# Grouped instance norm on one core: the middle units moved in pairs, with 64 KB rows instead of 32 KB rows

## The chip, the core and the metric

The kernel runs on one core of a Trainium2 chip. Times are device microseconds (us) of one execution; the time before is the median of three executions, 626.96 us (626.79 to 627.2). Beside them stands one profiled execution, from which all durations are taken.

## The reference

The input is 4 x 8 x 16 = 512 channels of 256 x 256 float32 numbers (134 MB), and a gamma for each of 8 x 16 = 128 channels. Every channel is normalized by its own mean and variance and multiplied by its gamma:

```
mu = x.mean(axis=(3, 4), keepdims=True)
var = ((x - mu) ** 2).mean(axis=(3, 4), keepdims=True)
x_norm = (x - mu) / np.sqrt(var + 1e-5)
out = x_norm * gamma[None, :, :, None, None]
```

## The kernel before, in words

A *unit* is 16 channels, laid on 128 partitions: 8 partitions (S) for each channel, 8192 numbers (32 KB) on each partition, 4 MB in all. There are 32 units, and DRAM holds the rows of a unit one behind the other, so that loading or storing a unit is one DMA of 128 rows of 32 KB. Such a DMA runs on all 16 DMA engines, eight rows on each, and each engine signals when its eight are done.

Six slots of SBUF (line 45, `AHEAD = 6`) hold six units. Unit u lies in slot u % 6, is normalized in place, and is stored from there; the load of unit u + 6 into the slot (line 136) waits for that store to land. I write L5 for the load of unit 5 and S5 for its store.

Which queue issues what: the first six loads go out at once, L1 and L3 from ScalarE's queue, the others from SyncE's (SP); all later loads go out from SP's queue, in order (lines 47-48, 56-57, 136); all stores from ScalarE's queue (line 134), so that a store is issued behind the work that ScalarE has before it. Each of the two queues is served in order, and both run on the same 16 DMA engines.

What is done with a unit (lines 105 to 136): VectorE sums each row (line 107) while ScalarE sums the squares (line 108; the squares themselves go to `junk`, which nobody reads); TensorE adds the partial sums of a channel's eight partitions and spreads them to all eight by a matmul with `navg` (line 116); VectorE, ScalarE and VectorE again make variance, root, reciprocal and scale on 128 x 1 tiles (lines 117 to 127); VectorE applies mean and scale to the whole unit (line 130); ScalarE's queue issues the store. VectorE takes the units strictly one after the other.

Before the loop, GpSimd's queue writes a small block of zeros (`touch`, 16 rows of 512 B) into the output (line 54), where the first store writes over it later, and loads gamma (line 55); 60 no-ops are asked for on ScalarE (lines 59-60); GpSimd makes `navg` (lines 66 to 75); VectorE spreads gamma to a row (line 83), and eight small matmuls and a copy turn it into columns, one for each unit of a group of eight (lines 87 to 94).

The order on each engine is the order of the program text (`manual_schedule`).

Of the kernel before, what the change touches and what calls it, by code (L numbers as in the profile page):

```python
# [1 line left out]

# [4 lines left out]

F32 = mybir.dt.float32
U8 = mybir.dt.uint8
ALU = mybir.AluOpType  # L10
ACTF = mybir.ActivationFunctionType
AX = mybir.AxisListType


@with_exitstack
def kernel(
    ctx: ExitStack,
    tc: tile.TileContext,
    x: bass.AP,
    gamma: bass.AP,  # L20
    out: bass.AP,
):
    nc = tc.nc
    B, G, C, H, W = x.shape
    P = nc.NUM_PARTITIONS
    HW = H * W
    n_ch = B * G * C
    S = 8
    K = P // S
    F = HW // S  # L30
    U = n_ch // K
    NG = (G * C) // K
    AHEAD = 6
    assert HW % S == 0 and (G * C) % K == 0

    xv = x.rearrange("b g c h w -> (b g c h w)").rearrange("(u p f) -> u p f", p=P, f=F)
    ov = out.rearrange("b g c h w -> (b g c h w)").rearrange("(u p f) -> u p f", p=P, f=F)
    gv = gamma.rearrange("g c -> (g c)")

    data = ctx.enter_context(tc.tile_pool(name="data", bufs=1))  # L40
    singles = ctx.enter_context(tc.tile_pool(name="singles", bufs=1))
    psum = ctx.enter_context(tc.tile_pool(name="psum", bufs=4, space=bass.MemoryType.PSUM))
    ctx.enter_context(tc.manual_schedule())

    slots = [data.tile([P, F], F32, name=f"xt{i}") for i in range(AHEAD)]

    def load(u, queue):
        queue.dma_start(out=slots[u % AHEAD][:], in_=xv[u])  # L48


    g_row = singles.tile([1, G * C], F32, name="g_row")
    touch = singles.tile([16, 128], F32, name="touch")
    nc.vector.memset(touch[:], 0.0)  # L53
    nc.gpsimd.dma_start(out=ov[0][0::S, 0:128], in_=touch[:])  # L54
    nc.gpsimd.dma_start(out=g_row[:], in_=gv[None, :])  # L55
    for u in range(AHEAD):
        load(u, nc.scalar if u in (1, 3) else nc.sync)

    for _ in range(60):
        nc.scalar.nop()  # L60

    eps_t = singles.tile([P, 1], F32, name="eps_t")
    nc.gpsimd.memset(eps_t[:], 1e-5)
    one = singles.tile([1, 1], F32, name="one")
    nc.gpsimd.memset(one[:], 1.0)
    navg = singles.tile([P, K, S], F32, name="navg")
    nc.gpsimd.memset(navg[:], -1.0 / HW)  # L67
    nc.gpsimd.affine_select(  # L68
        out=navg[:], in_=navg[:], pattern=[[-S, K], [0, S]], compare_op=ALU.is_ge,
        fill=0.0, base=0, channel_multiplier=1,  # L70
    )
    nc.gpsimd.affine_select(  # L72
        out=navg[:], in_=navg[:], pattern=[[S, K], [0, S]], compare_op=ALU.is_ge,
        fill=0.0, base=S - 1, channel_multiplier=-1,
    )
    navg_w = navg[:].rearrange("p k s -> p (k s)")
    root_eps = singles.tile([P, 1], F32, name="root_eps")
    nc.scalar.activation(out=root_eps[:], in_=eps_t[:], func=ACTF.Sqrt)  # L78
    g_rep = singles.tile([1, NG, K, S], F32, name="g_rep")
    g_ps = psum.tile([P, NG], F32, name="g_ps", bufs=1)  # L80
    g_col = singles.tile([P, NG], F32, name="g_col")

    nc.vector.tensor_copy(  # L83
        out=g_rep[:],
        in_=g_row[:].rearrange("o (n k) -> o n k", n=NG).unsqueeze(3).to_broadcast([1, NG, K, S]),
    )
    for n in range(NG):
        nc.tensor.matmul(  # L88
            out=g_ps[:, n : n + 1],
            lhsT=g_rep[:, n].rearrange("o k s -> o (k s)"),  # L90
            rhs=one[:],
            start=True, stop=True,
        )
    nc.vector.tensor_copy(out=g_col[:], in_=g_ps[:])  # L94

    junk = singles.tile([P, F], U8, name="junk")

    st = singles.tile([P, U, 2], F32, name="st")
    nvar = singles.tile([P, U], F32, name="nvar")
    std = singles.tile([P, U], F32, name="std")  # L100
    rstd = singles.tile([P, U], F32, name="rstd")
    scale = singles.tile([P, U], F32, name="scale")

    squares = []
    for u in range(U):
        t = slots[u % AHEAD]
        nc.vector.reduce_sum(out=st[:, u, 0:1], in_=t[:], axis=AX.X)  # L107
        square = nc.scalar.activation(  # L108
            out=junk[:], in_=t[:], func=ACTF.Square, accum_out=st[:, u, 1:2],
        )  # L110
        if u:

            tc.declare_no_dep(square.ins, squares[-1].ins, reason="junk, ordered by the root between")
        squares.append(square)
        ps = psum.tile([P, 2], F32, name="ps")
        nc.tensor.matmul(out=ps[:], lhsT=navg_w, rhs=st[:, u], start=True, stop=True)  # L116
        nc.vector.tensor_scalar(  # L117
            out=nvar[:, u : u + 1], in0=ps[:, 0:1], scalar1=ps[:, 0:1],
            scalar2=ps[:, 1:2], op0=ALU.mult, op1=ALU.add,
        )  # L120
        nc.scalar.activation(  # L121
            out=std[:, u : u + 1], in_=nvar[:, u : u + 1], func=ACTF.Sqrt,
            bias=eps_t[:], scale=-1.0,
        )
        nc.vector.reciprocal(out=rstd[:, u : u + 1], in_=std[:, u : u + 1])  # L125
        g = u % NG
        nc.vector.tensor_mul(  # L127
            out=scale[:, u : u + 1], in0=rstd[:, u : u + 1], in1=g_col[:, g : g + 1],
        )
        nc.vector.tensor_scalar(  # L130
            out=t[:], in0=t[:], scalar1=ps[:, 0:1], scalar2=scale[:, u : u + 1],
            op0=ALU.add, op1=ALU.mult,
        )
        nc.scalar.dma_start(out=ov[u], in_=t[:])
        if u + AHEAD < U:
            load(u + AHEAD, nc.sync)


# [1 line left out]
_INS = ['x', 'gamma']  # L140
_OUTS = [((4, 8, 16, 256, 256), 'float32')]


# [23 lines left out]
```

## Time and profile before

| | |
|---|---|
| median of three executions | 626.96 us |
| span of the profiled execution (its time outside of the span is not recorded) | 624.9 us |
| first and last data row on a DMA engine, from the span's start | 2.10 us, 623.90 us |
| moved | 268.46 MB in 64 transfers of 4 MB and two small ones |
| VectorE, ScalarE, TensorE busy | 71%, 38%, 3% of the span |
| one row of 32 KB on a DMA engine, median of 8192 | 1.213 us |

The profile's page gives the busy time of each engine, the span in 40 equal slices (the row named DMA is the busy share of the 16 DMA engines in tenths, 9 for 90% or more; below it what they moved), the queues (q1 is SP's, q10 ScalarE's, q0 GpSimd's), the groups of instructions, and how long the DMAs of each kind took from issue to landing. The trace also keeps a record of each row that a DMA engine moved, with queue, start, duration and size: 8192 rows of 32 KB, and 4-byte records, which are the signals that an engine's share of a DMA is done.

### The profile page before, as it was taken

The page shows a single profiled execution, that of the slowest core. Times are in us where ns is not written, and L with a number is a line of the kernel's source. Part 1 is how long each engine was busy: PE and PEld are TensorE (multiplying, and loading weights), DVE is VectorE, ACT ScalarE, POOL GpSimd, SP SyncE. Part 2 cuts the span into 40 slices and gives each one's busy share as a digit, 9 for nine tenths or more (in the row PEclk, how much of TensorE's full clock was granted, in tenths as well). Part 3 has the DMA queues.
Part 4 walks back from the last instruction along what each step waited for, and adds up shares of the span by engine and source line. Part 5 has one row for each costly group of instructions (what it writes and reads, how often), then busy time and mean ns, then how long its engine had stood idle before and what let it go on. Part 6 is the DMA issues. An engine that isn't in the chain of part 4 may idle for free.

```text
span 624.9 us, 631 instructions
## 1 busy us (share of the span) xinstructions
PE 21.4 (3%) x80; PEld 19.5 (3%) x80; DVE 443.4 (71%) x163; ACT 238.8 (38%) x98; POOL 2.4 (0%) x11
## 2 busy tenths in 40 slices
PE   0200000000000000000000000000000000000000
PEld 0200000000000000000000000000000000000000
DVE  0588999999776687666786767867668676687730
ACT  0444444444443234432344423444224442244400
POOL 1000000000000000000000000000000000000000
DMA  8999999999999999999999999999999999999998
GB/s 370 436 426 430 422 434 436 436 436 437 432 424 433 436 436 424 436 436 434 436 436 432 422 436 436 434 426 436 436 434 436 436 434 419 436 436 434 426 436 369
DMA packets 9282, 268.46 MB, mean 430 GB/s; under 512 B 1072, under 2 KB 1088, under 8 KB 1088
## 3 DMA queue, kind: packets, MB, share of 16 engines
q10 hardware_dynamic: 4896, 142.61, 52.9%
q1 hardware_dynamic: 4320, 125.83, 46.8%
q0 software_dynamic: 64, 0.01, 0.0%
q14 instruction: 2, 0.02, 0.0%
HBM read 134.22 MB, written 134.23 MB: 430 GB/s over the span
## 4 chain that ended last, share of the span: by engine, by line
another core or an unknown queue 61%; DMA 17%; DVE 15%; SPq 1%; PE 1%; issue 0%; ACT 0%
DVE st L107 10%; DMA xt<-in_x_dram 10%; DMA out_dram<-xt 8%; DVE xt L130 5%; SPq L48 1%; PE ps L116 1%; ACT std L121 0%; DVE nvar L117 0%; DVE rstd L125 0%; DVE scale L127 0%
## 5 line engine op out<-in xcount | busy, mean ns | idle before, releaser
L107 DVE TENSOR_REDUCE st<-xt 128x1 f32<-128x8192 f32 x32 | 277.9, 8685 | 100.4 <-DMA xt<-in_x_dram 100.4
L108 ACT ACTIVATE junk<-xt 128x8192 uint8<-128x8192 f32 x32 | 225.0, 7030 | 275.1 <-DMA xt<-in_x_dram 231.9
L130 DVE TENSOR_SCALAR xt<-xt,ps,scale 128x8192 f32<-128x8192 f32 x32 | 145.6, 4550 | 1.2
L121 ACT ACTIVATE std<-nvar,eps_t 128x1 f32<-128x1 f32 x32 | 9.4, 294 | 79.6 <-DVE nvar L117 79.6
L116 PE MATMUL ps<-st,navg 128*128 128x2 f32 x64 | 17.9, 349 | 557.1 <-DVE st L107 557.1
L116 PEld LDWEIGHTS ps<-st,navg 128*128 128x128 f32 x64 | 16.0, 311 | 558.9 <-issue 558.9
L117 DVE TENSOR_SCALAR nvar<-ps 128x1 f32<-128x1 f32 x32 | 9.2, 287 | 23.8 <-PE ps L116 23.8
L125 DVE RECIPROCAL rstd<-std 128x1 f32<-128x1 f32 x32 | 5.2, 164 | 11.6 <-ACT std L121 11.6
L83 DVE COPY g_rep<-g_row 1x1024 f32<-1x1024 f32 x1 | 0.7, 681 | 14.3 <-DMA g_row<-in_gamma_dram 14.3
L108 ACT ACTIVATION_READ_ACCUMULATOR junk<-xt 128x1 f32 x32 | 6.0, 186 | 0.0
L127 DVE TENSOR_TENSOR scale<-rstd,g_col 128x1 f32<-128x1 f32 x32 | 5.1, 159 | 1.1
L88 PE MATMUL g_ps<-one,g_rep 1*128 1x1 f32 x16 | 3.5, 347 | 16.1 <-DVE g_rep L83 16.1
L88 PEld LDWEIGHTS g_ps<-one,g_rep 1*128 1x128 f32 x16 | 3.5, 325 | 16.1 <-issue 16.1
L94 DVE COPY g_col<-g_ps 128x8 f32<-128x8 f32 x1 | 0.2, 166 | 3.7 <-PE g_ps L88 3.7
L78 ACT ACT_TABLE_LOAD x1 | 1.3, 1283 | 1.7 <-PEq L151 1.7
L53 DVE MEMSET touch<- 16x128 f32 x1 | 0.2, 165 | 0.9 <-PEq L151 0.9
L54 POOL DMA_DIRECT2D out_dram<-touch x1 | 0.6, 619 | 0.8 <-DVE touch L53 0.8
L55 POOL DMA_DIRECT2D g_row<-in_gamma_dram x1 | 0.5, 487 | 0.0
L68 POOL TENSOR_SCALAR_AFFINE_SELECT navg<-navg 128x128 f32<-128x128 f32 x1 | 0.4, 400 | 0.1
L72 POOL TENSOR_SCALAR_AFFINE_SELECT navg<-navg 128x128 f32<-128x128 f32 x1 | 0.4, 399 | 0.1
L67 POOL MEMSET navg<- 128x128 f32 x1 | 0.2, 232 | 0.0
L78 ACT ACTIVATE root_eps<-eps_t 128x1 f32<-128x1 f32 x1 | 0.2, 203 | 0.0
(6 smaller groups left out, 0.6 us busy)
## 6 DMA issues: line engine op xcount, KB each, us to landing
out_dram<-xt ACTq DMA_DIRECT2D x32, 4096.0 KB, 62.5
xt<-in_x_dram SPq DMA_DIRECT2D x30, 4096.0 KB, 38.5
xt<-in_x_dram ACTq DMA_DIRECT2D x2, 4096.0 KB, 31.5
out_dram<-touch POOLq DMA_DIRECT2D x1, 8.0 KB, 9.1
g_row<-in_gamma_dram POOLq DMA_DIRECT2D x1, 0.5 KB, 13.3
```

Source lines behind the costliest of these rows:

```text
L48: queue.dma_start(out=slots[u % AHEAD][:], in_=xv[u])
L78: nc.scalar.activation(out=root_eps[:], in_=eps_t[:], func=ACTF.Sqrt)
L83: nc.vector.tensor_copy(out=g_rep[:], in_=g_row[:].rearrange("o (n k) -> o n k", n=NG).unsqueeze(3).to_broadcast([1, NG, K, S]),)
L88: nc.tensor.matmul(out=g_ps[:, n : n + 1], lhsT=g_rep[:, n].rearrange("o k s -> o (k s)"), rhs=one[:], start=True, stop=True,)
L107: nc.vector.reduce_sum(out=st[:, u, 0:1], in_=t[:], axis=AX.X)
L108: square = nc.scalar.activation(out=junk[:], in_=t[:], func=ACTF.Square, accum_out=st[:, u, 1:2],)
L116: nc.tensor.matmul(out=ps[:], lhsT=navg_w, rhs=st[:, u], start=True, stop=True)
L117: nc.vector.tensor_scalar(out=nvar[:, u : u + 1], in0=ps[:, 0:1], scalar1=ps[:, 0:1], scalar2=ps[:, 1:2], op0=ALU.mult, op1=ALU.add,)
L121: nc.scalar.activation(out=std[:, u : u + 1], in_=nvar[:, u : u + 1], func=ACTF.Sqrt, bias=eps_t[:], scale=-1.0,)
L125: nc.vector.reciprocal(out=rstd[:, u : u + 1], in_=std[:, u : u + 1])
L127: nc.vector.tensor_mul(out=scale[:, u : u + 1], in0=rstd[:, u : u + 1], in1=g_col[:, g : g + 1],)
L130: nc.vector.tensor_scalar(out=t[:], in0=t[:], scalar1=ps[:, 0:1], scalar2=scale[:, u : u + 1], op0=ALU.add, op1=ALU.mult,)
```

## The change

The first six and the last six units stay as they are. The twenty between them become ten *wide* units: 32 channels, 4 partitions for each, 16384 numbers (64 KB) on each partition, 8 MB in one DMA of 128 rows of 64 KB. The six slots become three pairs of slots; a wide unit fills a pair, a narrow unit one half. There are 22 units now: 0 to 5 narrow, 6 to 15 wide, 16 to 21 narrow, and L and S count these from here on where the changed kernel is meant. A load is issued as soon as enough slots have been stored (`behind`): L6 behind S1, L7 behind S3, L8 behind S5, then L(u + 3) behind S(u) for wide ones, L16 and L17 behind S13, L18 and L19 behind S14, L20 and L21 behind S15.

A wide unit is summed in two halves on VectorE and ScalarE, and two matmuls add the halves in PSUM; the small steps, the apply (one instruction of 16384 numbers a partition) and the store come once for it. There are two `navg` matrices and two sets of gamma columns, one for each kind of unit. The block of zeros and the no-ops are gone.

```diff
-    slots = [data.tile([P, F], F32, name=f"xt{i}") for i in range(AHEAD)]
+    pairs = [data.tile([P, 2, F], F32, name=f"xt{i}") for i in range(SLOTS // 2)]
...
+    while at < total:
+        wide = 2 if ENDS <= at < total - ENDS else 1
+        units.append((at, wide, slot))
+        at += wide
+        slot = (slot + wide) % SLOTS
...
+    def on_chip(u):
+        at, wide, slot = units[u]
+        pair = pairs[slot // 2]
+        if wide == 2:
+            return pair[:].rearrange("p t f -> p (t f)")
+        return pair[:, slot % 2]
+
+    def in_dram(flat, u):
+        at, wide, slot = units[u]
+        return flat[at * K * HW : (at + wide) * K * HW].rearrange("(p f) -> p f", p=P)
...
     def load(u, queue):
-        queue.dma_start(out=slots[u % AHEAD][:], in_=xv[u])
-    touch = singles.tile([16, 128], F32, name="touch")
-    nc.vector.memset(touch[:], 0.0)
-    nc.gpsimd.dma_start(out=ov[0][0::S, 0:128], in_=touch[:])
+        queue.dma_start(out=on_chip(u), in_=in_dram(xf, u))
...
+    for u in range(U):
+        free += held[u]
+        while nxt < U and held[nxt] <= free:
+            free -= held[nxt]
+            behind[u].append(nxt)
+            nxt += 1
...
-    for _ in range(60):
-        nc.scalar.nop()
...
+    for wide in (1, 2):
+        s = S // wide
+        k = K * wide
+        ng = GC // k
+        m = singles.tile([P, k, s], F32, name=f"navg{wide}")
...
+        for h in range(wide):
+            part = t[:, h * F : (h + 1) * F]
+            nc.vector.reduce_sum(out=st[:, u, 2 * h : 2 * h + 1], in_=part, axis=AX.X)
+            square = nc.scalar.activation(
+                out=junk[:], in_=part, func=ACTF.Square, accum_out=st[:, u, 2 * h + 1 : 2 * h + 2],
+            )
...
+            nc.tensor.matmul(
+                out=ps[:], lhsT=navg[wide], rhs=st[:, u, 2 * h : 2 * h + 2],
+                start=h == 0, stop=h == wide - 1,
+            )
...
         nc.vector.tensor_scalar(
-            out=t[:], in0=t[:], scalar1=ps[:, 0:1], scalar2=scale[:, u : u + 1],
+            out=t, in0=t, scalar1=ps[:, 0:1], scalar2=scale[:, u : u + 1],
             op0=ALU.add, op1=ALU.mult,
         )
-        nc.scalar.dma_start(out=ov[u], in_=t[:])
-        if u + AHEAD < U:
-            load(u + AHEAD, nc.sync)
+        nc.scalar.dma_start(out=in_dram(of, u), in_=t)
+        for v in behind[u]:
+            load(v, nc.sync)
```

## The prediction, as it was put on record

> **What bounds the kernel now.** I read the page's slices first, then the stages, then the records of the single rows.
>
> ```profile
> PE 21.4 (3%) x80; PEld 19.5 (3%) x80; DVE 443.4 (71%) x163; ACT 238.8 (38%) x98; POOL 2.4 (0%) x11
> ...
> DMA  8999999999999999999999999999999999999998
> ...
> q10 hardware_dynamic: 4896, 142.61, 52.9%
> q1 hardware_dynamic: 4320, 125.83, 46.8%
> ...
> out_dram<-touch POOLq DMA_DIRECT2D x1, 8.0 KB, 9.1
> g_row<-in_gamma_dram POOLq DMA_DIRECT2D x1, 0.5 KB, 13.3
> ```
>
> No compute engine is full; the DMA engines are, from the first slice to the last, and the shares of q10 and q1 add up to 99.7%. The stages (us, busy time of PE, PEld, DVE, ACT, POOL, the clock's share, the DMA share, GB/s) say that no stage is different:
>
> ```profile
> 0.00:22.60 22.60, 3.54 (x16) 3.48 (x16) 1.01 (x3) 1.49 (x2) 2.40 (x11) 1.00 0.94 395
> 60.00:160.00 100.00, 3.92 (x14) 3.52 (x14) 89.46 (x36) 45.52 (x22) 0.00 (x0) 1.00 1.00 433
> 160.00:540.00 380.00, 11.15 (x40) 10.02 (x40) 274.16 (x100) 147.74 (x60) 0.00 (x0) 1.00 1.00 433
> 585.20:600.30 15.10, 0.56 (x2) 0.50 (x2) 13.85 (x5) 7.42 (x3) 0.00 (x0) 1.00 1.03 445
> ```
>
> So the time is 2.1 us to the first row, 621.8 us of full DMA engines, 1.0 us behind the last row: the span of 624.9; 2.05 us lie outside it up to the median of 626.96, which I carry over. A change can win only by making rows cheaper, and lose only by letting the DMA engines run dry. Where could they? At the end:
>
> ```profile
> 585.26 8.69 DVE L107 TENSOR_REDUCE st<-xt 128x1 f32<-128x8192 f32 x1 [4.35 <-DMA xt<-in_x_dram]
> 595.73 4.55 DVE L130 TENSOR_SCALAR xt<-xt,ps,scale 128x8192 f32<-128x8192 f32 x1
> 600.32 0.34 ACTq L134 DMA_DIRECT2D out_dram<-xt  x1
> ```
>
> The last load lands at 585.18; its unit is summed and applied, and its store goes out 15.1 us later. In the row records, stores land at 594.87, 604.55, 614.23 and 623.91: at 585.18 four stores were still to be moved, 9.68 us each. Three of them (29 us) cover the 15.1. **That cover is what the change touches.**
>
> In between, the row records show a load and a store landing together every 19.36 us: the two queues take turns, row by row, eight rows each, 19.36 / 16 = 1.21 us a row.
>
> **Is a turn a row, or so many bytes?** Each row of touch (512 B) took 27 ns, but its 4-byte signal ran 2.44 us after it, gamma's 32 B 2.42 us after that, its signal again 2.42: each time one 32 KB row of q1 and one of q10. That is also why 0.5 KB took 13.3 us to land. A queue with a small record loses its turn like one with 32 KB: turns go by record. The Trainium skill (DMA: Bandwidth & Descriptors, "Queues, rings and completion order") says the same, a round-robin that drains a whole packet before switching; it leaves open what a packet is for a 64 KB row, which no row here shows.
>
> **The change, part by part.**
>
> *Fewer, longer rows.* Twenty units of 8 + 8 rows an engine become 160 rows of 64 KB where there were 320 of 32 KB, and 20 signals an engine go: 180 records fewer. The fixed price of a record is not shown by itself. A whole 4-byte record takes 9 ns, so it is between 0 and 9 ns: 0 to 1.6 us won. I take the middle, 0.8 us. If records were waited for one by one, more would be won: by the fit of the Trainium skill (DMA: Bandwidth & Descriptors, "Anatomy of one DMA": about 2.0 us fixed for each DMA, plus bytes by 436 GB/s) twenty DMAs fewer would be worth 40 us. The trace disagrees: 8192 rows x 1.213 / 16 = 621 us fill the 621.8, so no fixed cost of a DMA is uncovered.
>
> *Wide stage.* L(u + 3) waits for S(u). A wide unit needs 38.7 us of load and 38.7 of store at half rate, and on VectorE 2 x 8.69 + 1.75 for the small chain + 2 x 4.55 = 28.2: together 105.6 against three pairs x 38.7 = 116, so one of the queues always has rows. VectorE (28.2 of 38.7), ScalarE (2 x 7.2) and TensorE stay beneath; the second half's square waits for the first on the same engine, nothing. Cost 0; cover gone at 10 us.
>
> *Entering it.* L6, L7 and L8 wait for two stores each, so q1 runs empty for some us before L8; q10 has S5, S6 queued, and one queue alone moves as much (0.98 to 1.03 DMA share behind 585.2, where q10 is alone). Cost 0. It fixes a phase, though: L8 is issued 0.41 us after S5 lands (row records to SP's issue) and a first row follows an issue by 1.3 to 2.2 us (0.80 to 2.10 and 2.97 at the start), while S6 starts at once with a 2.42 us row. Most engines give S6 two rows first, so when S6 lands, L8 still lacks two. From there they go in step: L(u + 2) lands 7.3 us after S(u).
>
> *Leaving it.* Now a 64 KB store row takes turns with 32 KB load rows, and stores get two thirds. From S13's landing, with 1.21 and 2.42 us a row:
> - L, S, L: L15 lands at 7.3. Then S14's other seven rows with six of L16: 24.2, S14 lands at 31.4.
> - S15 goes out 28.3 us after L15: 35.6, first row about 37.3; meanwhile five load rows alone. Eight rows of S15 with eight load rows: 29.0, S15 lands at 66.4. 19 load rows done of the 48 of L16 to L21.
> - 29 load rows and 28 store rows in turn, 57 x 1.21 = 69.0: L21 lands at 135.4. Of S16 to S20, 12 rows are left: 14.5 us, empty at 149.9.
> - S21 goes out at 135.4 + 15.1 = 150.5, first row 1.3 to 2.2 later. **All 16 engines are dry for 1.9 to 2.8 us**; the last one counts, so 2.8.
>
> Before, the 15.1 us had 29 us of cover; now 14.5.
>
> *Touch and no-ops.* ScalarE's issues end at 1.68 and its table load starts at 1.72: the 60 no-ops take nothing, nor does dropping them. Touch cost each engine 36 ns. Whether it warms the output for the first store is not shown; with it, the load rows beside S0's first took 1.6 to 1.9 instead of 1.21 us (41.58 us), and the first load rows of all 1.2 to 2.0. So dropping it costs -0.04 to 0.8 us; I take 0, since that delay stands already in the trace. S0 no longer waits for touch, which landed 27 us earlier.
>
> *Small work.* Three more instructions on GpSimd (1.0 us), 4 more gamma matmuls (0.44 us each with their weights, 1.8) and two copies: the chain ended at 19.9 and would at most end at 22.4, still before the first load (22.55); gamma also comes two turns earlier. If late, VectorE would start late, and S0 queues behind L3 till 41.98 anyway. In the loop 10 x 4 small VectorE and ScalarE steps go; they stand beside full DMA engines: 0.
>
> **Sum:** +2.8 (dry end) - 0.8 (records) = +2.0 on a span of 624.9, so 626.9, and 626.96 + 2.0 = **629.0**.
>
> **Rivals.**
> - *No overtaking.* A 64 KB row is cut into two records of 32 KB, or turns go by bytes: then the change does not do what it says, or does it without its price. Stores and loads stay level, at the last landing four stores are left as before, nothing runs dry: 626.96 - 0.1 (20 signals at most 9 ns) to - 0.8, 626.2 to 626.9. For it: all rows shown have one size. Against it: the 512 B and 4 B records that waited full turns. 0.20.
> - *Faster.* No overtaking, and each record that goes saves all of the 9 ns: 625.3. A 4-byte record would then be fixed price alone, which is the far end. 0.08. (That DMAs have a fixed cost which nothing covers, and so end far lower, gets no chance: it needs idle DMA engines, and there are none to 0.7 us in 621.8.)
> - *One row less of phase.* If L8's first row comes within S6's first 2.42 us on all engines (an arrival of 1.7 to 2.6 us, so some surely will not), one load row is left instead of two. Then S15 follows S14 almost at once, 17 load rows are done instead of 19, 31 are left against 30 store rows, S20 has 10 rows left: 12.1 us of cover, 4.3 to 5.2 us dry, 626.96 + 5.2 - 0.8 = 631.4. 0.10.
> - *Something slower that no row shows*, a 64 KB row that takes more than two of 32 KB: 1% more on 160 rows of 2.42 would be 3.9 us, on top. All 8192 rows but 83 took 1.205 to 1.230, so nothing points at it. 0.07.
>
> **How the numbers follow.** The forecast has 0.55, from 627.8 (a row more of cover, 1.21) to 630.2 (a row less). A measurement of this kernel can tell about 0.2%, 1.25 us: faster is beneath 625.7, slower above 628.2. Faster: 0.09. Same: no overtaking and the low edge of the forecast, 0.24. Slower: 0.67. The range, 625.7 to 631.5, takes in the forecast, the phase rival and no overtaking, and leaves out 0.15.
>
> **What would show it.** Right: records of 64 KB with about 2.42 us each; in the row records S14 and S15 landing some 30 us apart where wide stores before them are 38.7 apart; the last load landing 12 to 13 us later than 585.2; a DMA share well beneath 1 for some 3 us before the last store; the last store issued after the one before it has landed. Wrong: records of 32 KB alone; S14, S15 at 38.7; four stores left behind the last load; a dry stretch in the wide stage; 64 KB rows over 2.43 us; a first store whose rows take several us.

## The result, and the profile after

The changed kernel is slower: 638.34 us, median of four executions (634.03 to 639.94), beside 626.88; the ratio is 1.0171 with a 95% interval of 1.0143 to 1.0199. Six executions taken later give 637.78 (634.1 to 640.42) and 1.0169 (1.0146 to 1.0191). Executions of the kernel before lie within 0.8 us, those of the changed one within 6: already that points to something not repeatable at its end. The execution that was profiled took 639.94 us, the slowest of the four.

One thing about times: the row records, here and in the text ahead, are given 0.30 us later than on the profile's own clock (there the first row before starts at 1.80 us, not 2.10). Distances between rows are not touched by it, and the landings given here lie mostly within 0.1 us of the time at which their semaphore was seen. A distance from an issue to a first row is 0.30 us too long in the prediction (1.0 to 1.9 us, not 1.3 to 2.2); below, such distances are on the profile's clock.

The page of the changed kernel, span, slices, queues:

```profile
span 638.2 us, 566 instructions
...
DMA  9999999999999999999999999999999999999966
GB/s 380 442 394 433 450 413 409 454 448 421 423 448 427 431 436 427 431 439 411 456 398 460 407 448 444 411 452 407 448 417 429 417 419 407 435 429 429 431 301 265
...
q10 hardware_dynamic: 3456, 142.61, 51.9%
q1 hardware_dynamic: 2880, 125.83, 46.4%
```

Before, only the first and the last slice were under 9; now the last two stand at 6, and 301 and 265 GB/s were moved there. The records fell from 4896 and 4320 to 3456 and 2880: there are rows of 64 KB, as the change says, and the wide ones took 2.418 us in the median.

The stages of the changed kernel, cut at what the prediction named (S13 lands at 469.5, S14 at 501.1, S15 at 538.6, L21 at 610.8; the last column but one is the share of the DMA engines):

```profile
197.00:469.50 272.50, 7.83 (x28) 7.03 (x28) 186.94 (x42) 101.78 (x35) 0.00 (x0) 1.00 1.00 432
469.50:501.00 31.50, 1.12 (x4) 1.00 (x4) 25.37 (x6) 14.54 (x5) 0.00 (x0) 1.00 0.96 409
501.00:538.60 37.60, 1.11 (x4) 1.00 (x4) 27.81 (x11) 14.83 (x6) 0.00 (x0) 1.00 1.00 415
538.60:610.80 72.20, 1.67 (x6) 1.50 (x6) 42.75 (x16) 22.25 (x9) 0.00 (x0) 1.00 1.00 432
610.80:627.00 16.20, 0.56 (x2) 0.50 (x2) 13.85 (x5) 7.42 (x3) 0.00 (x0) 1.00 0.49 209
```

The last row is the one that matters. Before, the same 15 us between the last load and the last store's issue ran at a full share; here the DMA engines are half empty. The last narrow unit, in the timeline of the changed kernel:

```profile
610.91 8.69 DVE L154 TENSOR_REDUCE st<-xt 128x1 f32<-128x8192 f32 x1 [4.89 <-DMA xt<-in_x_dram]
...
621.39 4.55 DVE L178 TENSOR_SCALAR xt<-xt,ps,scale 128x8192 f32<-128x8192 f32 x1
...
625.97 0.34 ACTq L182 DMA_DIRECT2D out_dram<-xt  x1
```

S20 has landed at 624.15, 1.8 us before S21 is issued: the dry end that was forecast. What was not forecast stands in the row records. Here is when the first and the last of the 16 engines finished their share of a transfer:

```
                       first engine   last engine   apart
before, L31 (last load)      584.28        585.18    0.90
after,  L6                   115.56        117.49    1.93
after,  L17                  517.04        524.70    7.66
after,  L21 (last load)      601.13        610.84    9.71
after,  S20                  616.96        624.15    7.19
after,  S21 (last store)     636.86        637.02    0.16
```

A load has landed when the last engine is done. The records do not name their engine; rows are strung together by end and start to tell the 16 apart. One engine lags, and everything behind it waits: that engine is dry for 3.0 us (624.15 to 627.11), the typical one, done with S20 at 617 to 619, for some 9.

### The profile page after: what moved, and what is told of

It reads as the page before. It is cut to its first block, busy times and chain, and to the rows that moved or that the text cites. A ratio compares the mean times of both kernels' runs of the same rounds, so it can differ in the third digit from the quotient of the medians.

```text
span 638.2 us, 566 instructions
## 1 busy us (share of the span) xinstructions
PE 23.3 (4%) x88; PEld 21.3 (3%) x88; DVE 434.1 (68%) x124; ACT 235.9 (37%) x88; POOL 3.1 (0%) x13
## 3 DMA queue, kind: packets, MB, share of 16 engines
q10 hardware_dynamic: 3456, 142.61, 51.9%
q1 hardware_dynamic: 2880, 125.83, 46.4%
## 4 chain that ended last, share of the span: by engine, by line
DMA 59%; DVE 34%; another core or an unknown queue 2%; PE 1%; ACT 1%; issue 1%; SPq 0%
DMA xt<-in_x_dram 32%; DMA out_dram<-xt 27%; DVE st L154 22%; DVE xt L178 11%; PE ps L161 1%; ACT std L169 1%; DVE nvar L165 1%; DVE rstd L173 0%; DVE scale L175 0%; SPq L71 0%
## 5 line engine op out<-in xcount | busy, mean ns | idle before, releaser
L178 DVE TENSOR_SCALAR xt<-xt,ps,scale 128x8192 f32<-128x8192 f32 (+1 forms) x22 | 142.8, 6490 | 0.8
L169 ACT ACTIVATE std<-nvar,eps_t 128x1 f32<-128x1 f32 x22 | 6.5, 294 | 69.3 <-DVE nvar L165 69.3
L165 DVE TENSOR_SCALAR nvar<-ps 128x1 f32<-128x1 f32 x22 | 6.3, 287 | 16.4 <-PE ps L161 16.4
L173 DVE RECIPROCAL rstd<-std 128x1 f32<-128x1 f32 x22 | 3.6, 164 | 8.0 <-ACT std L169 8.0
L130 PE MATMUL g_ps<-one,g_all 1*128 1x1 f32 x24 | 5.4, 348 | 11.9 <-DVE g_all L125 11.9
L130 PEld LDWEIGHTS g_ps<-one,g_all 1*128 1x128 f32 x24 | 5.3, 324 | 11.9 <-issue 11.3
L175 DVE TENSOR_TENSOR scale<-rstd,g_col 128x1 f32<-128x1 f32 x22 | 3.5, 159 | 0.7
```

The costliest lines, as they stand in the source:

```text
L130: nc.tensor.matmul(out=g_ps[:, n : n + 1], lhsT=g_rep[:, n].rearrange("o k s -> o (k s)"), rhs=one[:], start=True, stop=True,)
L165: nc.vector.tensor_scalar(out=nvar[:, u : u + 1], in0=ps[:, 0:1], scalar1=ps[:, 0:1], scalar2=ps[:, 1:2], op0=ALU.mult, op1=ALU.add,)
L169: nc.scalar.activation(out=std[:, u : u + 1], in_=nvar[:, u : u + 1], func=ACTF.Sqrt, bias=eps_t[:], scale=-1.0,)
L175: nc.vector.tensor_mul(out=scale[:, u : u + 1], in0=rstd[:, u : u + 1], in1=g_cols[wide][:, g : g + 1],)
L178: nc.vector.tensor_scalar(out=t, in0=t, scalar1=ps[:, 0:1], scalar2=scale[:, u : u + 1], op0=ALU.add, op1=ALU.mult,)
```

## The experiments

Theory A is the forecast's: 64 KB store rows take two turns' worth of bytes beside 32 KB load rows, the loads fall behind while the wide stage is left, and the end runs dry. Rivals: B, pairs as such (a load that waits for two units); C, 64 KB rows are bad wherever they stand; D, the entry sets it.

**All rows 32 KB, pairs kept (e1).** The halves of a pair get 32 bytes between them, so that a wide row cannot be moved in one piece:

```diff
-    pairs = [data.tile([P, 2, F], F32, name=f"xt{i}") for i in range(SLOTS // 2)]
+    pairs = [data.tile([P, 2, F + 8], F32, name=f"xt{i}") for i in range(SLOTS // 2)]
...
-            return pair[:].rearrange("p t f -> p (t f)")
-        return pair[:, slot % 2]
+            return pair[:, :, 0:F]
+        return pair[:, slot % 2, 0:F]
```

> The changed kernel with each half of a pair of slots 32 bytes apart on the partition, so that every wide transfer keeps its place, its waits and its bytes but moves in rows of 32 KB instead of 64 KB. Theory A (a 64 KB store row against a 32 KB load row takes two thirds of the DMA engines, loads fall behind where the wide stage is left, and the last unit's store is late): all rows alike, no overtaking, four stores left behind the last load, 626 to 628.5. Theory B (pairs as such: a load waits for two units' stores, its queue runs empty, whatever the rows): 634 or more. Theory C (64 KB rows are slower or put the 16 engines out of step wherever they stand): 626 to 628.5, as A.

Measured: 629.91 (628.76 to 630.09), ratio 1.0043 (1.0028 to 1.0058). Some 8 of 11 us come back, so row size is most of the loss; 2.8 us stay, more than A allowed, with all rows alike.

**The two stores that meet narrow loads in 32 KB rows (e2).** The helper `parts` cuts a wide transfer into two, one half of each partition's row after the other:

```diff
+    cut_loads = ()
+    cut_stores = (14, 15)
+
+    def parts(u, cut):
+        return (slice(0, F), slice(F, 2 * F)) if cut else (slice(None),)
...
-        nc.scalar.dma_start(out=in_dram(of, u), in_=t)
+        for c in parts(u, u in cut_stores):
+            nc.scalar.dma_start(out=in_dram(of, u)[:, c], in_=t[:, c])
```

> The changed kernel, but the stores S14 and S15, the two wide ones that meet narrow loads, go out as two transfers of 32 KB rows each, one half of every partition's row after the other; the other eight wide units keep 64 KB rows. Theory A: the overtaking is gone where it costs, nearly the whole loss comes back, 626.5 to 630. Theory B: 634 or more. Theory C: at most the two units' share of the loss comes back, 634 or more.

Measured: 630.48 (629.49 to 633.39), ratio 1.0064 (1.0044 to 1.0084). Two stores of 22 bring back 7 to 8 us, though the median lies just over A's 630. The stretch between the last load (589.22, the engines 0.9 us apart) and the issue of the last store, in this kernel's stages:

```profile
589.20:604.30 15.10, 0.56 (x2) 0.50 (x2) 13.78 (x5) 7.42 (x3) 0.00 (x0) 1.00 1.02 437
```

The share is full again. So most of the loss hangs on the leaving of the wide stage, and rows of 64 KB elsewhere cost little between these medians (0.6 us beside e1): this speaks for A, against B, and leaves C a small part at most. It does not separate the dry end from slower rows, since both go together here; e7 does. What is left, 3.4 us, is about what e1 left.

**The three loads that meet narrow stores in 32 KB rows (e3).** `cut_loads = (6, 7, 8)`, nothing else.

> The changed kernel, but the loads L6, L7 and L8, the wide ones that meet narrow stores where the wide stage is entered, go out as two transfers of 32 KB rows each; leaving the wide stage is untouched. Theory A: the loss stays, 633 to 640. Theory B: it stays, 633 to 640. A theory D, that the delay and the phase of the entry set the loss (S6 lands 197 us where 192 was worked out): below 632.

Measured: 655.73 (650.04 to 661.46), ratio 1.0489 (1.0434 to 1.0544): none of the theories. The slices of its page show where it went, 160 to 230 us:

```profile
GB/s 388 421 421 421 453 421 431 443 421 439 352 373 336 354 388 453 429 429 437 425 453 392 437 453 433 408 453 437 412 441 418 437 427 402 445 425 429 443 327 265
```

The entry itself became smooth (each half of L6 to L8 waits for one store only, and loads and stores land together each 19.4 us until 158.8). Then S6 and S7, in 64 KB rows beside the cut loads, took 3.1 us a row in the mean instead of 2.42, for 70 us. So D is not settled by it, but one thing is: cutting rows on one queue alone can be worse than on none.

**The kernel before without the block of zeros and the no-ops (e4).**

```diff
-    touch = singles.tile([16, 128], F32, name="touch")
-    nc.vector.memset(touch[:], 0.0)
-    nc.gpsimd.dma_start(out=ov[0][0::S, 0:128], in_=touch[:])
...
-    for _ in range(60):
-        nc.scalar.nop()
```

> The kernel before without the block of zeros and without the no-ops, nothing else changed. The prediction has this part at 0 (between -0.04 and 0.8 us): 626.9, at most 627.7. Were the block what keeps the first store quick: over 628.

Measured: 627.2 (626.66 to 627.53), ratio 1.0001 (0.9991 to 1.0010). This part is 0.

**Both ends cut (e5).** `cut_loads = (6, 7, 8)`, `cut_stores = (6, 7, 14, 15)`: no wide row stands beside a narrow one.

> The changed kernel with 32 KB rows, as two transfers of one half each, wherever a wide transfer meets a narrow one: loads L6, L7, L8 (each half then waits for one narrow store only, so that the load queue does not run empty at the entry), stores S6 and S7, which meet those loads, and S14 and S15. From L9 and S8 to L15 and S13 rows stay at 64 KB on both queues. If the loss comes from rows of unlike size side by side and from the entry's empty load queue, both are gone: 626 to 628. If 64 KB rows by themselves cost (slow, or out of step), six wide units still have them: 630 or more.

Measured: 631.05 (630.17 to 631.87), ratio 1.0059 (1.0042 to 1.0075). The slow rows of e3 are gone, since S6 and S7 are cut too, and the end is not dry; yet 4 us stay; by what was expected, that is the side of 64 KB rows that cost by themselves. The row records tell why it is no clean test: the engines are 0.6 us apart until the second half of L8 lands at 197.6; then L9, still one transfer, waits for both halves of S6, the load queue is empty for some 4 to 8 us, and from there the engines are 2 to 8 us apart, 3.8 at the last store. The empty queue has only been moved. Against their median length, rows are longer by 1.3 us on the mean engine where L9 starts, and by 1.6 us from there to 470 us: the empty queue and the 64 KB rows each have a part.

**All in halves (e6).** `cut_loads` and `cut_stores` are `range(6, 16)`; a half of a load waits for its own slot alone.

> The changed kernel with every wide transfer as two of 32 KB rows, one half each; a wide load's halves wait for one slot each. Beside the all-32-KB-rows kernel with whole wide transfers (629.9) it tells what the entry is: if that kernel's 2.8 us are the load queue's running empty on entering the wide stage, this one has none of them, 626.5 to 627.8; if they are the computing in pairs or the pairs' waits later on, it stays at 629 to 631.

Measured: 627.68 (627.31 to 627.86), ratio 1.0008 (0.9998 to 1.0017). With 32 KB rows, e1 beside e6 differs in the entry (and in the finer waits behind it): 2.2 us. Computing in pairs costs nothing that can be measured. In e6 a load and a store land together each 19.36 us from 42 to 585.66, as in the kernel before.

**The last unit's sums cut short (e7, and again as e11).** Its statistics are taken over 512 of 8192 numbers a partition, so that S21 goes out earlier:

```diff
             part = t[:, h * F : (h + 1) * F]
+            if u == U - 1:
+                part = part[:, :512]
```

> The changed kernel, but the sums and squares of the last narrow unit are taken over 512 of its 8192 numbers a partition, so that its statistics are not those of the channel and its store goes out some 8.2 us earlier. If the dry end is all of the loss, the last store starts when the typical engine is empty, and 8 us come back: 630. If, as the trace has it, the slowest engine is dry for 3.0 us only and the rest of the loss is that engine's lag behind the others, 3 us come back: 634 to 637. If the end is not dry at all for the engine that sets it: no change, 638.

Measured: 634.06 (632.06 to 635.8), ratio 1.0110 (1.0084 to 1.0137). From the last load's landing on, the stage that was half empty is full up to the end (the share is under 1 only for the 1.2 us behind the last row and for up to 2.8 us in which most engines are done and one is not):

```profile
604.90:631.20 26.30, 0.56 (x2) 0.50 (x2) 5.85 (x5) 1.02 (x3) 0.00 (x0) 1.00 0.86 372
```

S20 lands at 620.34 and S21 at 630.02, 9.68 us later, and so do their first engines (617.50, 627.18): nothing is dry any more, and the time is still 7 us over the kernel before. Both kernels once more, on one chip:

> The changed kernel once more, for a baseline on the same chip as the next one and for how far its executions differ from each other: 634 to 640, median about 638. If the end waits for one lagging engine, the spread goes with the lag, so the executions stay several us apart where those of the kernel before are 0.7 us apart.

> The kernel with the last narrow unit's sums taken over 512 of 8192 numbers a partition (its statistics are not those of the channel) once more, now beside the changed kernel on the same chip: 3 to 5 us faster than that if the dry end is the part that the prediction had (2.8), 8 or more if the dry end is all.

Measured: 637.78 (634.1 to 640.42) and 634.68 (632.74 to 638.1). The medians are 3.1 us apart here, 4.3 the first time; the means of all ten and all nine executions are 3.0 us apart, with a 95% interval of 1 to 5. In the second profile of the changed kernel the lagging engine is dry from 622.2 to 625.2, 3.0 us. So the dry end is of the size that was forecast, and it is about 3 of the 11 us.

**Transfers alone (e8, e9).** No norm is computed; a constant is stored from one pair of slots while loads run into the two others, both queues full (in e9 only up to 167 us).

```diff
+    stages = [(1, 1, 8), (2, 2, 4), (2, 1, 4), (1, 2, 8)]
...
+            nc.sync.dma_start(out=chip, in_=dram(xf, at_load % 30, wide_load))
...
+            nc.scalar.dma_start(out=dram(of, at_store, wide_store), in_=source[:, : wide_store * F])
```

> No norm is computed: only transfers, stores of a constant from one pair of slots beside loads into the two other pairs, both queues always full, in four stages: 32 KB rows on both queues; 64 KB on both; 64 KB store rows beside 32 KB load rows; 32 KB store rows beside 64 KB load rows. If turns go by row, stages 3 and 4 have two bytes of the one queue to one of the other. If unlike rows side by side are slow by themselves, 64 KB store rows take 2.9 to 3.4 us in stage 3, as beside the cut loads of the entry, and 2.42 in stage 2. If they are slow only in another circumstance, 2.42 in all stages. Time about 660 us by 1.21 us for each 32 KB, up to 700 with slow rows.

Measured: 676.69 us. When the first and the last engine had done their share of a load:

```
rows of store / load   landings, first engine            landings, last engine
32 KB / 32 KB           82.27 101.63 121.00              83.27 102.63 121.99     each 19.36
64 KB / 64 KB          199.56 238.20 276.84             200.56 240.28 278.98     each 38.6
64 KB / 32 KB          306.09 335.09 364.09 393.09      309.72 341.85 372.54 403.21
32 KB / 64 KB          498.16 527.16 556.16             510.84 539.84 568.84     each 29.00
```

Eight rows of 64 KB beside eight of 32 KB take 29.0 us: turns go by row, and the queue with long rows gets two thirds. That is theory A's premise by itself. The Trainium skill (DMA: Bandwidth & Descriptors, "Queues, rings and completion order") has a round-robin that drains a whole packet of one queue before it switches, a packet being some 9 to 17 descriptors as a rule. The trace agrees with the round-robin; its turn here is a single row of up to 64 KB, since eight rows of one queue alternate with eight of the other. And in the third stage, the engines drift apart, from 2.1 to 10.1 us: fourteen keep 29.0 us, two take 30.6 to 32.1. On those two, rows are longer at times, up to 3.1 us for a 64 KB store row. In the fourth stage, with the sizes exchanged, the distance stays at 12.7 and does not grow.

> No norm is computed: only transfers as in the earlier stages of transfers alone, now with the loads of the cut entry. Stage 1: 64 KB store rows beside loads of half a wide unit, 32 KB out of every 64 KB of DRAM; stage 2: 64 KB store rows beside whole narrow units, 32 KB rows one behind the other; stage 3: halves on both queues; stage 4: stage 1 again with other addresses. Where loads L6 to L8 were cut, 64 KB store rows beside such halves took 2.9 to 3.4 us on all engines. If it is the place of the rows in DRAM (both queues step by 64 KB), stage 1 and 4 show 2.9 to 3.4 and stage 2 shows 2.42. If it is rows of unlike size on engines that are in step, stages 1 and 2 show it. If it needs the compute engines at work, none does. Output rows of stage 3 hold a constant as all others.

Measured: 514.86 us, no computing; in stage 1, 64 KB store rows beside halves, all 16 engines kept 29.00 us for 8 + 8 rows and stayed 0.54 us apart. So neither the place of the halves in DRAM nor rows of unlike size on engines in step bring about the slow rows of e3 by themselves; what they need besides is open. Later in this run, from 210 us on, engines drifted apart here too, from 0.5 to 10; by then the store queue had begun to run empty between its stores, so this part is no test with full queues.

## Why the prediction was wrong, point by point

The direction was right, and so were the turns by row and the dry end; the size was not: 629.0 forecast, at most 631.5; 638.3 measured. What failed are the steps that put rows at one length on all engines, so that entering the wide stage, the wide stage and leaving it cost nothing beyond the dry end. Against the medians, what each part was given and what it took:

| part | forecast | measured | from |
|---|---|---|---|
| fewer, longer records | -0.8 | -0.9 in the row records, not visible in a time | below |
| entering the wide stage | 0 | about +2.2 | e1 beside e6 |
| wide stage | 0 | +1.6 on the mean engine, 2.5 on the lagging one, in one execution | row records |
| dry end | +2.8 | about +3 (medians 3.1 and 4.3 apart) | e11, e7 beside the changed kernel |
| unlike rows, beyond the dry end | not thought of | about +4, a remainder | e2 (7.5 in all) less the dry end |
| touch, no-ops, small work | 0 | 0 (e4); computing in pairs -0.1 to 1.1 (e6) | ratios to the kernel before |

Entry, dry end and unlike rows add up to about 10 of 11 us between medians, from which the wide stage cannot be separated; what is missing is within what two medians of kernels that scatter by 6 us can differ.

The row records close the sum for the profiled execution, whose last row ends 13.1 us later than the one before (637.02, 623.91). On the engine that lags, rows are in all 12.6 us longer than their medians of 1.213 and 2.418 us: 1.3 at the start, 1.6 at the entry (78 to 120 us), 2.5 in the wide stage (197 to 470), 7.1 behind it. In the kernel before, it is 1.3 on the engine that ends last, nearly all at the start, with 0.3 idle. The difference, 11.0, with 3.0 dry and 0.9 saved, is the 13.1. On the mean engine rows are 6.8 us longer in all, 1.3 before: all engines have long rows, and the one that lags nearly twice the mean.

- *Fewer, longer rows.* From the start of a 32 KB row to the start of the next it is 1209.4 ns in the mean, of a 64 KB row 2414.1: some 5 ns saved for each of 160 pairs, 0.75 us, and 20 signals of 6 ns. (The fit of the Trainium skill that the prediction sets beside this term stands on its page for DMAs issued by GpSimd; these come from SP and ScalarE.) The term was right, and it drowns: with 64 KB rows in the wide stage e2 is no faster than e1 without any (630.48, 629.91).
- *Wide stage.* Never dry (share 1.00), and VectorE not the bound: right. But the cost of 0 was not: of its 908 load rows of 64 KB, 158 took more than 2.43 us, up to 2.97, spread over all 16 engines. That was one of the prediction's own signs of being wrong, and a busy engine hides it.
- *Entering it.* **This step failed.** I took the time from issue to first row from the start of the run, where the DMA engines were idle, and put the cost of the empty queue at 0. The changed kernel's L6, in its timeline:

```profile
81.66 0.33 SPq L71 DMA_DIRECT2D xt<-in_x_dram  x1
```

Its first rows start 4.5 to 7.0 us after that (86.47 to 88.91 in the row records), on an empty queue beside a full one; the store rows just before took up to 1.9 us instead of 1.21 and the first load rows 3.0 to 4.2 instead of 2.42. No engine was idle, so the share of 1.00 hides it. In e1, whose rows are all 32 KB, this stretch has 1.5 us of such excess on the mean engine, beside 0.01 before, and the 16 engines finish the last store 3.0 us apart (623.98 to 627.00) instead of 0.9. e6, where the queue never empties, has neither. That the empty queue is the cause is shown by the pair e1 and e6 only as far as both differ in nothing else that costs; e5, where it was moved to L9, agrees. The queue ran empty before L7 and L8 as well, and their first rows came 3.7 to 5.7 us behind the issue, but no rows were longer there (0.01 us on the mean engine, beside 1.26 at L6). So an empty queue can cost and does not always; why is open.
- *Leaving it.* The row-by-row working nearly holds for the stores: S14 lands 31.6 us behind S13 (31.4 worked out), S15 37.5 behind S14 (35.0). The phase does not: at S6, 10 of the 16 engines had two rows of L8 left, as forecast, and 6 had one, but they did not stay in step, and at S13, 14 engines had one row of L15 left, so that L15 landed 4.8 us behind S13, not 7.3. **The step that failed is that it was worked out for one engine as if all went alike.** The last load was to land 69.0 us behind S15's landing; it took 72.2, and in all it landed 12.8 us later than the forecast's 598. Of these, 6.9 were there when S13 landed (469.5; 598 less 135.4 is 462.6), from the entry and the wide stage. By the engines, the first was 3.1 us late at L21, and the rest is the lag of the last, 7.7 us behind the first at L17 and 9.7 at L21. In e2, with S14 and S15 cut, the lag at the last load is 0.9 us. That unlike rows can make single engines lag is shown by e8, without any computing; why those engines, and why not in e9's first stage, is open. Since the records do not name engines, whether it is the same ones each time is not known.
- *The dry end.* Right for the engine that sets it, 3.0 us by two profiles beside 2.8, but in part by luck: that engine had 11 rows of S16 to S20 left at L21's landing (13.3 us), not 12 (14.5), and S21's first row came 1.1 us behind the issue as the prediction counts it, not 2.2. That the others stand empty for 9 costs nothing more, as e7 shows: not 8 us came back.
- *The rivals.* "No overtaking" did not happen: the records have 64 KB, turns go by row (e8). "One row less of phase" (0.10) describes what most engines did from S8 on; the last engine came out between it and the forecast, with 11 rows left where they had 10 and 12, and neither has the long rows. "Something slower that no row shows" was nearest to what was missed and had 0.07. It was priced as every 64 KB row a little longer; in the median they are not (2.418 us, two of 32 KB 2.426), but 255 of 2560 took more than 2.43 us, on all engines, and what that added differs from engine to engine. The range left it out.

## What to carry to other kernels

When both DMA queues were full, a queue's share was set by the length of its rows (e8), so let transfers that run side by side have rows of one size, above all near the end, where late loads turn into a dry end. DMA engines that look busy can still lose time: look at how far apart they finish a transfer, since a landing waits for the last one, and at single rows that are longer than the median. A coarser unit makes a queue run empty where it meets finer ones; where that had a price here, it came in longer rows at the refill, not in idle time.

## What the runs showed of the hardware that I had not expected

- A load issued into an empty queue beside a full one started 3.7 to 7.0 us later (L6 to L8 in the changed kernel); with idle DMA engines it was 0.8 to 1.9 us (S21 in the changed kernel: issued at 625.97, first row at 626.81 on the same clock).
- Two of 16 engines fell behind by 1.5 to 3.1 us for each 8 + 8 rows while 64 KB store rows ran beside 32 KB load rows, the other fourteen by nothing (e8). In the changed kernel's wide stage, with 64 KB rows on both queues, it was the load rows that were longer, and hardly a store row (141 of 908 and 1 of 892 by more than 0.03 us).
- 64 KB store rows of 3.1 us in the mean for 70 us (e3), in a circumstance that transfers alone did not bring about (e9). Not settled.
